# The output projection of a decoder layer in seven products of quarters per 1024 columns

## The chip, the cores and the metric

The kernel runs on one core of a Trainium2 chip. The metric is the device time of one execution in microseconds (us). [...]

## The reference, cut to what matters

One layer of a decoder on 512 tokens of width 2048. `D_IN` is 7184 columns, `w_out` is 2048 x 2048, all in float32.

```python
h = rms_norm(x, norm_g) * (1 + scale) + shift            # scale, shift, gate from c @ w_ada
z = h @ w_in
u_a, v_a, g_a, q_b, k_b, v_b, g_b, f_b = jnp.split(z, pts, axis=-1)
y_a = chunked_spatial_gating(gelu(u_a), gelu(v_a), ...) * silu(g_a)      # branch A, 1024 wide
y_b = forgetting_attention(q_b, k_b, v_b, f_b, b_f) * silu(g_b)          # branch B, 16 heads, 1024 wide
y = jnp.concatenate([y_a, y_b], axis=-1) @ w_out
return rms_norm(x + gate * y, final_g)
```

## The kernel before

**Precision.** Every float32 operand of a large product is split in two parts: `hi`, a rounded copy written by ACT (`split`, L65, or `w_tile`, L117), and `lo`, the source minus `hi`, written by DVE (or by POOL where `eng`/`loeng` says so). A product of a and b is three matmuls: hi·hi, lo·hi and hi·lo. A weight tile is therefore: a DMA into a `raw` tile (four buffers in all), an ACT copy into `whi`, a subtraction into `wlo` (two buffers each), and then the matmuls that use it.

**Tiles.** The activations lie with channels on the 128 partitions: `hh[k]`, `hl[k]` are block k (of 16) of h, 128 x 512 tokens. `mm_cols` makes 128 output columns x 512 tokens, `mm_toks` 128 tokens x up to 512 columns. A PSUM bank holds 128 x 512 sums; there are four of kind `mm`, and four that small work and attention share (`x`).

**Order of the program.** A first stage (L358) makes u_A and most of g_A while `w_ada` arrives. Then come groups of columns: `v_group` (v_B), `qk_group` and `g_group` (g_B) for four heads at a time, u = 0 to 3. Then the values of branch A (`va`, L689), the rest of its gate (`ga`, L764) and the output projection (L808).

Work that is not a large product hangs on two lists. `tick()` (L133) is called after each weight tile: it takes one entry of `slots` (the attention of the four heads before, later the mixing of branch A: `norm_half`, `mix_head`, `split_y`) and one entry of `fillers` (`gate_step`: POOL multiplies and adds up the adaLN gate, L584). The scheduler then sets the order of each engine's stream from the dependencies and priorities; weight tiles have a raised priority.

**Output projection.** For each of three groups of 512 columns, eight weight tiles of two channel blocks each (128 x 2 x 512) meet all four token tiles: 24 matmuls of 128 x 512 per weight tile. The weights of the fourth group are loaded ahead (`load_w3`) and used token tile by token tile (L823), so that the final norm of one token tile runs under the matmuls of the next. `wo_evac` multiplies by the gate (DVE, from PSUM), adds x (DVE), squares (ACT) and multiplies by `final_g` (DVE). The last lines scale by the norm and write out.

Of the kernel before, what the change touches and what calls it, by code (L numbers as in the profile page):

```python
# [27 lines left out]
def trunk_kernel(  # L28
# [281 lines left out]
    for kb in range(KB):  # L310
# [5 lines left out]
        xk = act.tile([P, S], F32, tag="y", name=f"xT{kb}")  # L316
# [32 lines left out]
    def new_y(b):  # L349
        y[b] = act.tile([P, S], F32, tag="y", name=f"y{b}")  # L350
# [111 lines left out]
    def attention_slots(u):  # L462
# [62 lines left out]
        def values(i):  # L525
# [16 lines left out]
            nc.vector.scalar_tensor_tensor(tm[a], op[a], 0.5, tm[a], ALU.mult, ALU.add)  # L542
            nc.vector.tensor_tensor(y[8 + b][a], tm[a], sgb[b][a], ALU.mult)
# [61 lines left out]
    bias2 = gp_.tile([P, 8, P], F32, name="bias2")  # L605
# [66 lines left out]
    v_group(0)  # L672
    qk_group(0)
    g_group(0)
    for u in range(1, 4):
        if u == 1:
            fillers.append(spatial_weights)
            for g in range(4):
                for i in range(8):
                    fillers.append(lambda g=g, i=i: gate_step(g, i))  # L680
                    if g and i == 2:
                        fillers.append(lambda g=g: gate_sum(g - 1))
            fillers.extend([lambda: None] * 3 + [lambda: gate_sum(3)])
# [60 lines left out]

    yh, yl = [None] * KB, [None] * KB

    def split_y(k):
        yh[k] = act.tile([P, S], F32R, tag="hh", name=f"yh{k}")
        yl[k] = act.tile([P, S], F32R, tag="hl", name=f"yl{k}")
        split(yh[k], yl[k], y[k], nc.gpsimd if k in (1, 3, 5, 7) else None)  # L750

    norm_half(0)
    c_ = lambda f, *a: (lambda: f(*a))
    slots.extend([
        [],
        [c_(mix_head, 0), c_(mix_head, 1)],
        [c_(mix_head, 2), c_(mix_head, 3)],
        [c_(norm_half, 1)],
        [c_(split_y, 0), c_(split_y, 1)],
        [c_(mix_head, 4), c_(mix_head, 5), c_(split_y, 2), c_(split_y, 3)],  # L760
        [c_(mix_head, 6), c_(mix_head, 7), c_(split_y, 4), c_(split_y, 5)],
        [c_(split_y, 6), c_(split_y, 7)],
    ])
# [112 lines left out]
```

## Time and profile before

| | |
|---|---|
| median of 3 runs | 920.67 us (920.17 to 920.79) |
| the profiled execution | 922.11 us, of which the span is 920.4 us |
| busy in the span | PE 898.9, DVE 528.7, ACT 412.4, POOL 326.4 us |
| mean granted clock of PE | 0.988 |
| read and written | 142.74 MB, mean 155 GB/s |

Busy time of PE counts a matmul from its start to its modelled end; consecutive matmuls overlap, so the pace has to be read from the distance between starts. All rows of the profile are of the one profiled execution, whose span is 0.3 us under the median.

### The profile page before, as it was taken

Reading aid. Unit: us, or ns where it says so; the run is one execution under the profiler, and the core shown is the slowest. Engines: PE = TensorE matmul, PEld = TensorE weight load, DVE = VectorE, ACT = ScalarE, POOL = GpSimd, SP = SyncE. Lnnn points to the kernel's source line nnn. Section 1 sums busy time; section 2 is a strip of 40 time slices with the busy share of each in tenths; the row PEclk is TensorE's granted clock in tenths of the full one; section 3 lists DMA queues with packets and bytes.
Section 4 is the critical chain, followed back from the end, with each engine's and each line's share of the span. In section 5 each row is a group of like instructions: output and inputs, shape, how many; then the busy total and the mean of one; then the engine's idle time right before and its main releaser. Section 6 shows DMA issues by size and latency. Waiting matters only on the chain.

```text
span 920.4 us, 12414 instructions
## 1 busy us (share of the span) xinstructions
PE 898.9 (98%) x4504; PEld 763.0 (83%) x4504; DVE 528.7 (57%) x886; ACT 412.4 (45%) x724; POOL 326.4 (35%) x238
## 2 busy tenths in 40 slices
PE   6999999999999999999999999999999999999995
PEld 4888888898888878988889888998888888888884
DVE  5678888364644685656645644555525884355522
ACT  5553323535464653654546544665514423233211
POOL 1366555531004997687897800000000230000000
PEclk8899999999999999999999999999999999999999
DMA  9999995234333454444556423223233233455222
GB/s 341 352 353 355 354 302 189 76 89 136 94 114 115 130 170 145 154 150 127 160 172 179 144 81 107 78 70 92 71 107 97 81 125 105 149 180 196 69 104 92
DMA packets 113821, 142.74 MB, mean 155 GB/s; under 512 B 8400, under 2 KB 85408, under 8 KB 113248
## 3 DMA queue, kind: packets, MB, share of 16 engines
q1 hardware_dynamic: 113328, 141.39, 48.5%
q8 instruction: 35, 0.57, 0.2%
q10 hardware_dynamic: 432, 0.57, 0.2%
q14 instruction: 26, 0.21, 0.1%
HBM read 137.54 MB, written 4.19 MB: 154 GB/s over the span
## 4 chain that ended last, share of the span: by engine, by line
PE 95%; DMA 2%; issue 1%; DVE 1%; ACT 0%; SPq 0%; POOLq 0%; POOL 0%; ACTq 0%; DVEq 0%
PE s L145 6%; PE s L147 6%; PE s L146 6%; PE wo L156 5%; PE wo L154 5%; PE wo L155 5%; PE vb L155 3%; PE vb L156 3%; PE vb L154 3%; PE k L145 3%; PE k L147 3%; PE gb L145 3%; PE gb L146 3%; PE k L146 3%; PE va L156 3%; PE gb L147 3%
## 5 line engine op out<-in xcount | busy, mean ns | idle before, releaser
L593 POOL TENSOR_SCALAR gate<-gate,sc 128x512 f32<-128x512 f32 x60 | 104.4, 1750 | 37.4 <-DMA gate<-in_w_ada_dram 34.5
L130 POOL TENSOR_TENSOR wlo_st<-raw_st,whi_st 128x1024 fp32r<-128x1024 f32 (+3 forms) x36 | 68.5, 1904 | 59.6 <-ACT whi_st L129 55.7
L145 PE MATMUL s<-hh,whi_st 128*128 128x512 f32 x224 | 88.0, 396 | 1.4 <-ACT hh L267 1.4
L146 PE MATMUL s<-hl,whi_st 128*128 128x512 f32 x224 | 88.1, 393 | 0.0
L594 POOL TENSOR_TENSOR gate<-gate,gate 128x512 f32<-128x512 f32 x60 | 86.5, 1442 | 2.1
L244 DVE SCALAR_TENSOR_TENSOR acc<-ada,sc,acc 128x512 f32<-128x512 f32 x98 | 73.9, 755 | 5.8 <-DMA ada<-in_w_ada_dram 3.1
L147 PE MATMUL s<-hh,wlo_st 128*128 128x512 f32 x224 | 76.4, 395 | 0.0
L154 PE MATMUL wo<-whi_wo,yh 128*128 128x512 f32 x192 | 74.8, 390 | 0.0
L155 PE MATMUL wo<-whi_wo,yl 128*128 128x512 f32 x192 | 74.7, 389 | 0.0
L155 PE MATMUL vb<-whi_vb,hl 128*128 128x256 f32 (+1 forms) x256 | 72.1, 287 | 0.0
L154 PE MATMUL vb<-whi_vb,hh 128*128 128x256 f32 (+1 forms) x256 | 71.8, 286 | 0.0
L156 PE MATMUL wo<-wlo_wo,yh 128*128 128x512 f32 x192 | 70.0, 390 | 0.0
L156 PE MATMUL vb<-wlo_vb,hh 128*128 128x256 f32 (+1 forms) x256 | 67.7, 285 | 0.0
L91 POOL TENSOR_TENSOR rsv<-rsv,nhalf 128x1 f32<-128x1 f32 x4 | 4.6, 1150 | 166.1 <-DVE rsv L90 166.1
L129 ACT ACTIVATE whi_st<-raw_st 128x1024 fp32r<-128x1024 f32 (+3 forms) x36 | 31.2, 870 | 66.3 <-PE s L146 40.9
L841 POOL TENSOR_TENSOR sfin<-sfin,nhalf 128x1 f32<-128x1 f32 x4 | 2.2, 549 | 149.0 <-DVE sfin L838 149.0
L145 PE MATMUL k<-hh,whi_k 128*128 128x512 f32 x128 | 51.1, 399 | 1.8 <-DVE q L445 1.8
L145 PEld LDWEIGHTS s<-hh,whi_st 128*128 128x128 f32 x224 | 42.6, 191 | 10.1 <-ACT hh L267 1.5
L146 PE MATMUL q<-hl,whi_q 128*128 128x512 f32 x128 | 50.7, 396 | 0.0
L145 PE MATMUL q<-hh,whi_q 128*128 128x512 f32 x128 | 50.4, 394 | 0.0
L146 PE MATMUL gb<-hl,whi_gb 128*128 128x512 f32 x128 | 50.3, 393 | 0.0
L145 PE MATMUL gb<-hh,whi_gb 128*128 128x512 f32 x128 | 50.3, 393 | 0.0
(227 smaller groups left out, 2363.8 us busy)
## 6 DMA issues: line engine op xcount, KB each, us to landing
ada<-in_w_ada_dram SPq DMA_DIRECT2D x128, 256.0 KB
gate<-in_w_ada_dram SPq DMA_DIRECT2D x32, 512.0 KB
raw_wo<-in_w_out_dram SPq DMA_DIRECT2D x24, 512.0 KB
raw_q<-in_w_in_dram SPq DMA_DIRECT2D x16, 512.0 KB
raw_k<-in_w_in_dram SPq DMA_DIRECT2D x16, 512.0 KB
raw_gb<-in_w_in_dram SPq DMA_DIRECT2D x16, 512.0 KB
raw_va<-in_w_in_dram SPq DMA_DIRECT2D x16, 512.0 KB
raw_st<-in_w_in_dram SPq DMA_DIRECT2D x21, 384.0 KB
```

Source lines behind the costliest of these rows:

```text
L91: nc.gpsimd.tensor_tensor(dst, dst, nhalf[:, 0:1], ALU.pow)
L129: nc.scalar.activation(hi, raw, AF.Copy)
L130: (loeng or nc.vector).tensor_tensor(lo, raw, hi.bitcast(F32), ALU.subtract)
L145: nc.tensor.matmul(pt, hi[:, j, cs], hh[k], start=(k == first), stop=False)
L146: nc.tensor.matmul(pt, hi[:, j, cs], hl[k], start=False, stop=False)
L147: nc.tensor.matmul(pt, lo[:, j, cs], hh[k], start=False, stop=(k == last))
L154: nc.tensor.matmul(o, ah[k][:, tsl], hi[:, j, :], start=(k == first), stop=False)
L155: nc.tensor.matmul(o, al[k][:, tsl], hi[:, j, :], start=False, stop=False)
L156: nc.tensor.matmul(o, ah[k][:, tsl], lo[:, j, :], start=False, stop=(k == last))
L244: nc.vector.scalar_tensor_tensor(sb if kk == KB - 1 else a, ga[:, j], col, a, ALU.mult, ALU.add)
L593: nc.gpsimd.tensor_scalar(ga[:, j], ga[:, j], sc[:, kk : kk + 1], None, ALU.mult)
L594: nc.gpsimd.tensor_tensor(a, a, ga[:, j], ALU.add)
```

## The change

**The projection in quarters.** Split y by tokens (first 256, last 256) and by channels (branch B's 1024, branch A's 1024), and w_out by the same channels and by two groups of 512 columns. A plain product of 2 x 2 quarters takes eight products of quarters; the scheme used takes seven, with sums and differences of the quarters on both sides. One run of it (`unit(u)`) makes 1024 columns (groups g1 = 2u and g2 = 2u+1), and there are two. Each product is four weight tiles of two channel blocks, and each tile serves two token tiles: 12 matmuls per tile, 48 per product.

| product | left side (activations) | weights, per tile |
|---|---|---|
| p1, into banks V | `A11`: branch B, first tokens | one tile of w_out |
| p7, into Z | `S3`: branch B, last minus first | difference T of two tiles |
| p6, into X | `S2` = S3 + branch A, last tokens | a tile minus T |
| p5, into Z | `S1` = S2 + branch B, first | a tile minus T |
| p2, into V | `A12`: branch A, first | one tile |
| p4, into X | `A22`: branch A, last | T minus the tile of p2 |
| p3, into Z | `S4`: branch A, first, minus S2 | one tile |

The sums of activations are made by POOL (`split_b`, `sums`), in place of the tiles `y`, and split once more. The differences of weights (`minus`) are made half by DVE, half by POOL; where a tile is used as loaded (p1, p2, p3) one of its two `lo` halves goes to POOL. Results are copied or added out of PSUM (`c1`, `c7`, `u2`, `u3`), multiplied by the gate (`gated`), x is added by POOL (`residual`), and the squares go to ACT. p1 of both units comes first, then the rest of unit 0, then unit 1, whose p3 is done token tile by token tile at the end.

**Branch A earlier.** `va_products` now stands right behind the first stage, and its mixing in the slots of `v_group(0)`. g_B of the last four heads moves behind `ga`. The gate of heads 12 to 15 is multiplied in later (`late`).

The diff, cut to its core:

```diff
+    def va_products(): ...        # the former loop over va, as a function
+    fillers.append(spatial_weights)
+    va_products()
+    slots.extend([
+        [c_(norm_half, 0)],
+        [c_(mix_head, 0), c_(mix_head, 1)],
+        [c_(mix_head, 2), c_(mix_head, 3)],
+        [c_(norm_half, 1)],
+        [c_(mix_head, 4), c_(mix_head, 5)],
+        [c_(mix_head, 6), c_(mix_head, 7)],
+    ])
     v_group(0)
     ...
-        g_group(u)
+        if u < 3:
+            g_group(u)
...
+    def split_b(i):
+        b = y[8 + i]
+        nc.gpsimd.tensor_tensor(b[:, hi_half], b[:, hi_half], b[:, lo_half], ALU.subtract)
+        split_y(8 + i)
+    def sums(i):
+        b, a = y[8 + i], y[i]
+        nc.gpsimd.tensor_tensor(b[:, hi_half], b[:, hi_half], a[:, hi_half], ALU.add)
+        nc.gpsimd.tensor_tensor(b[:, lo_half], b[:, lo_half], b[:, hi_half], ALU.add)
+        ...
+        split(sh_[i], sl_[i], b)
+        nc.gpsimd.tensor_tensor(b[:, lo_half], a[:, lo_half], b[:, hi_half], ALU.subtract)
+        s4[i] = act.tile([P, 2, H], F32R, name=f"s4_{i}", tag="ya", bufs=8)
+        split(s4[i][:, 0], s4[i][:, 1], b[:, lo_half])
...
+    def wsplit(src, name, eng=None):
+        ...
+        for j in range(2):
+            split(hi[:, j, :], lo[:, j, :], src[:, j, :], eng if j else None)
+        return hi, lo
+    def mm_part(bank_, kind, i, tt, hi, lo, begin, end):
+        h_, l_ = lhs(kind, i, tt)
+        nc.tensor.matmul(bank_, h_, hi, start=begin, stop=False, skip_group_check=True)
+        nc.tensor.matmul(bank_, l_, hi, start=False, stop=False, skip_group_check=True)
+        newest_mm[0] = nc.tensor.matmul(bank_, h_, lo, start=False, stop=end, skip_group_check=True)
+    def residual(rr, t, g, src=None, eng=None):
+        xr = pb.tile([P, 512], F32, name=f"xr{g}_{t}", tag="sgB", bufs=3)
+        nc.sync.dma_start(xr, x[0, t * P : (t + 1) * P, g * 512 : (g + 1) * 512])
+        (eng or nc.gpsimd).tensor_tensor(rr, rr, xr, ALU.add)
+        return xr
+    def piece(rr, t, g, fin=True):
+        xr = residual(rr, t, g)
+        squares(rr, t, g, xr)          # ACT; xr is free only after it
+        if fin:
+            nc.vector.tensor_tensor(rr, rr, fgs[g], ALU.mult)
...
+        def w_raw(half, g, name):
+            return lambda i: wsplit(raw(half, g, name, i), f"{name}_{u}_{i}", nc.gpsimd)
+        def minus(dst, a, b):
+            for j in range(2):
+                (nc.gpsimd if j else nc.vector).tensor_tensor(
+                    dst[:, j, :], a[:, j, :], b[:, j, :], ALU.subtract
+                )
+            return dst
...
+        product(V, "A11", w_raw(1, g1, "p1"), True, range(3))
+        yield
+        product(V, "A11", w_raw(1, g1, "p1"), True, [3])
+        ...
+        yield
+        product(Z, "S3", w_p7, True)
+        ...
+        product(X, "S2", w_p6, True)
+        ...
+        both(lambda t: nc.gpsimd.tensor_tensor(u3[t], u2[t], c7[t], ALU.add))
+        both(lambda t: nc.gpsimd.tensor_tensor(c7[t], c7[t], c1[t], ALU.add))
+        product(Z, "S1", w_p5, True)
+        ...
+        for i in range(4):
+            product(V, "A12", w_p2, False, [i])
+            product(X, "A22", w_p4, False, [i])
+        ...
+            product(Z, "S4", w_raw(0, g2, "p3"), False)       # unit 0; unit 1: by token tile
```

Where the instructions stand now is shown at three places. The first is POOL. Before, these are the last rows of its stream that work on whole tiles: the four values of branch A (`vl`) and four blocks of y, and from there to the end of the kernel only four instructions of 128x1 (`sfin`):

```order
L91 TENSOR_TENSOR rsv_6452<-rsv_6452,nhalf 128x1
L67 TENSOR_TENSOR yl_6764<-y_1730,yh_6763 128x512
L67 TENSOR_TENSOR vl_1_6663<-va_1_5764,vh_1_6662 128x512
L67 TENSOR_TENSOR vl_1_6668<-va_1_5766,vh_1_6667 128x512
L67 TENSOR_TENSOR vl_1_6673<-va_1_5768,vh_1_6672 128x512
L67 TENSOR_TENSOR vl_1_6678<-va_1_5770,vh_1_6677 128x512
L67 TENSOR_TENSOR yl_6834<-y_1734,yh_6833 128x512
L67 TENSOR_TENSOR yl_6904<-y_1738,yh_6903 128x512
L67 TENSOR_TENSOR yl_6942<-y_1811,yh_6941 128x512
L841 TENSOR_TENSOR sfin<-sfin,nhalf 128x1 x4
```

Now POOL works through the whole projection; this piece is unit 0 around the end of p6 (`ta`, `tb`, `tc` hold T, L912 is `minus`, L973 and L974 the sums into `u3` and `c7`, L869 is `residual`):

```order
L912 TENSOR_TENSOR tc_7065<-b_0_3_7254,tc_7065 128x512
L912 TENSOR_TENSOR p_0_0_7286<-p_0_0_7286,ta_7063 128x512
L912 TENSOR_TENSOR p_0_1_7308<-p_0_1_7308,ta_7063 128x512
L912 TENSOR_TENSOR p_0_2_7330<-p_0_2_7330,tb_7064 128x512
L912 TENSOR_TENSOR p_0_3_7352<-p_0_3_7352,tc_7065 128x512
L973 TENSOR_TENSOR u_0_7278<-u_0_7276,c_0_7182 128x512
L973 TENSOR_TENSOR u_1_7279<-u_1_7277,c_1_7183 128x512
L912 TENSOR_TENSOR ta_7063<-p_0_0_7390,ta_7063 128x512
L974 TENSOR_TENSOR c_0_7182<-c_0_7182,c_0_7023 128x512
L974 TENSOR_TENSOR c_1_7183<-c_1_7183,c_1_7024 128x512
L912 TENSOR_TENSOR ta_7063<-p_0_1_7430,ta_7063 128x512
```

POOL had nothing of 128x512 behind the mixing; from p1 to the end it now has 82 instructions of 128x512 and 10 of 128x256, every one with two inputs in SBUF.

The second place is DVE. Before, in the second group of the projection, one subtraction of 128x1024 per weight tile (24 matmuls):

```order
L130 TENSOR_TENSOR wlo_wo_12_7170<-raw_wo_12_7167,whi_wo_12_7169 128x1024
L130 TENSOR_TENSOR wlo_wo_14_7200<-raw_wo_14_7197,whi_wo_14_7199 128x1024
L130 TENSOR_TENSOR wlo_wo_0_7230<-raw_wo_0_7227,whi_wo_0_7229 128x1024
L130 TENSOR_TENSOR wlo_wo_2_7260<-raw_wo_2_7257,whi_wo_2_7259 128x1024
L67 TENSOR_TENSOR w3l_7418<-raw_w_0_7415,w3h_7417 128x1024
```

Now p7 and the start of p6 of unit 0 (an `x2` is the two halves of one tile):

```order
L912 TENSOR_TENSOR ta_7063<-b_0_1_7100,b_0_1_7102 128x512
L67 TENSOR_TENSOR wlo_p_0_1_7107<-ta_7063,whi_p_0_1_7106 128x512 x2
L912 TENSOR_TENSOR tb_7064<-b_0_2_7134,b_0_2_7136 128x512
L67 TENSOR_TENSOR wlo_p_0_2_7141<-tb_7064,whi_p_0_2_7140 128x512 x2
L912 TENSOR_TENSOR tc_7065<-b_0_3_7158,b_0_3_7160 128x512
L912 TENSOR_TENSOR ta_7063<-b_0_0_7188,ta_7063 128x512
L67 TENSOR_TENSOR wlo_p_0_3_7165<-tc_7065,whi_p_0_3_7164 128x512 x2
```

Three instructions of 128x512 with two inputs in SBUF now stand for 12 matmuls, where one of 128x1024 stood for 24.

The third place is SP between p3 of unit 0 (`p_0_*_76xx`) and p7 of unit 1 (`b_1_*`). Before, in the same part of the program, the loads of x (`xr`) stood among the weights of the projection too:

```order
L790 DMA xr_0_7075<-in_x_dram 128x512
L790 DMA xr_1_7081<-in_x_dram 128x512
L123 DMA raw_wo_8_7107<-in_w_out_dram 128x2x512
L790 DMA xr_2_7087<-in_x_dram 128x512
L790 DMA xr_3_7093<-in_x_dram 128x512
L123 DMA raw_wo_10_7137<-in_w_out_dram 128x2x512
```

Now:

```order
L868 DMA xr_3_7571<-in_x_dram 128x512
L825 DMA b_1_0_7675<-in_w_out_dram 128x2x512
L868 DMA xr_0_7660<-in_x_dram 128x512
L825 DMA b_1_0_7677<-in_w_out_dram 128x2x512
L868 DMA xr_1_7665<-in_x_dram 128x512
L825 DMA b_1_1_7699<-in_w_out_dram 128x2x512
L868 DMA xr_2_7964<-in_x_dram 128x512
L825 DMA b_1_1_7701<-in_w_out_dram 128x2x512
```

Each `xr` has one of three buffers (tag `sgB`), free again when ACT has squared an earlier piece, so the weights of p7 behind it are issued only after the pieces of unit 0 have gone through POOL and ACT.

More of the change, by code (lines that the diff above doesn't have):

```diff
@@ L315, in trunk_kernel @@
             )
-        xk = act.tile([P, S], F32, tag="y", name=f"xT{kb}")
+        xk = act.tile([P, S], F32, tag="ya" if kb < 8 else "yb", bufs=8, name=f"xT{kb}")
         with ExitStack() as es:
@@ L349, in new_y @@
     def new_y(b):
-        y[b] = act.tile([P, S], F32, tag="y", name=f"y{b}")
+        y[b] = act.tile([P, S], F32, tag="ya" if b < 8 else "yb", bufs=8, name=f"y{b}")
     def evac_g(b, pt, pool):
@@ L670, in qk_group @@
         slots.extend(attention_slots(u))
[L672 to L683, printed above, removed]
-        g_group(u)
-        qk_group(u)
-        v_group(u)
@@ L743, in mix_head @@
         nc.vector.tensor_tensor(y[h], y[h], mt, ALU.mult)
-    yh, yl = [None] * KB, [None] * KB
+    fillers.append(spatial_weights)
[8 more added lines that the diff above has]
+    ])
+    v_group(0)
+    heads_tiles()
+    qk_group(0)
+    g_group(0)
+    for u in range(1, 4):
+        if u == 1:
+            for g in range(4):
+                for i in range(8):
+                    fillers.append(lambda g=g, i=i: gate_step(g, i))
+                    if g and i == 2:
+                        fillers.append(lambda g=g: gate_sum(g - 1))
+            fillers.extend([lambda: None] * 3 + [lambda: gate_sum(3)])
+        if u < 3:
+            g_group(u)
+        qk_group(u)
+        v_group(u)
+    H = S // 2
+    yh, yl = [None] * KB, [None] * KB
+    sh_, sl_, s4 = [None] * 8, [None] * 8, [None] * 8
+    lo_half, hi_half = slice(0, H), slice(H, S)
+    def split_b(i):
+        b = y[8 + i]
+        nc.gpsimd.tensor_tensor(b[:, hi_half], b[:, hi_half], b[:, lo_half], ALU.subtract)
+        split_y(8 + i)
     def split_y(k):
@@ L823, in trunk_kernel @@
[L823 to L836 removed]
+    fga = pb.tile([P, 2, 512], F32, name="fga", tag="fs")
@@ new lines, in trunk_kernel, with wtile, wget @@
+    nc.sync.dma_start(
+        fga.rearrange("p a n -> p (a n)"),
+        final_g[0:1024].rearrange("(a n) -> a n", a=1).broadcast_to([P, 1024]),
+    )
+    fgs = {0: fga[:, 0, :], 1: fga[:, 1, :]}
+    def wtile(name):
+        return wp.tile([P, 2, 512], F32, tag="raw", name=name, bufs=4)
+    def wget(dst, half, g, i):
+        k = 8 * half + 2 * i
+        nc.sync.dma_start(dst, wout_r[:, k : k + 2, g * 512 : (g + 1) * 512])
+        return dst
+    def wsplit(src, name, eng=None):
+        hi = wp.tile([P, 2, 512], F32R, tag="whi", name=f"whi_{name}")
+        lo = wp.tile([P, 2, 512], F32R, tag="wlo", name=f"wlo_{name}")
+        for j in range(2):
+            split(hi[:, j, :], lo[:, j, :], src[:, j, :], eng if j else None)
+        return hi, lo
@@ new lines, in product, with gated @@
+    def product(banks, kind, weights, begin, steps=range(4)):
+        for i2 in steps:
+            with tc.high_priority(offset=WPRI):
+                hi, lo = weights(i2)
+            for j in range(2):
+                for tt in range(2):
+                    i = 2 * i2 + j
+                    mm_part(banks[tt], kind, i, tt, hi[:, j, :], lo[:, j, :], begin and i == 0, i == 7)
+            tick()
+    def gated(rr, src, g):
+        nc.vector.tensor_tensor(rr, src, gate[:, g, :], ALU.mult)
@@ L852 @@
+    units = [unit(0), unit(1)]
+    for z in units + units:
+        next(z)
+    for z in units:
+        for _ in z:
+            pass
 _INS = ["x", "c", "norm_g", "w_ada", "b_ada", "w_in", "ln_v_g", "ln_v_b", "w_s", "b_s", "b_f", "w_out", "final_g"]
```

295 lines of the change are left out of this document (180 added, 115 removed).

## The prediction

> **What bounds the kernel now.** I read the page's shares first, then the chain of waits.
>
> ```profile
> PE 898.9 (98%) x4504; PEld 763.0 (83%) x4504; DVE 528.7 (57%) x886; ACT 412.4 (45%) x724; POOL 326.4 (35%) x238
> PE 95%; DMA 2%; issue 1%; DVE 1%; ACT 0%; SPq 0%; POOLq 0%; POOL 0%; ACTq 0%; DVEq 0%
> ```
>
> The chain is PE for 95% of the span, so time goes where matmuls go. Their pace comes from the chain in order of time: the same row returns once per weight tile of 24 matmuls.
>
> ```profile
> 771.18 0.45 PE wo L156 x2
> 776.62 0.45 PE wo L156 x2
> ```
>
> 5.44 us for 24 is 0.2267 us per 128x512 matmul. Then the groups by shape, for counts and unit prices, and two stretches of the span:
>
> ```profile
> L154 PE MATMUL wo<-whi_wo,yh 128*128 128x512 f32 x192 | 74.8, 390 | 0.0
> L833 PE MATMUL wo<-w3h,yh 128*128 128x512 f32 x64 | 24.9, 389 | 0.0
> L785 DVE TENSOR_TENSOR r<-wo,gate 128x512 f32<-128x512 f32 x16 | 10.9, 688 | 29.9 <-PE wo L835 24.5 <-PE wo L156 5.4
> L66 ACT ACTIVATE yh<-y 128x512 fp32r<-128x512 f32 x16 | 10.0, 629 | 22.0 <-DVE y L743 19.2 <-PE ga L147 2.6
> ...
> L130 POOL TENSOR_TENSOR wlo_st<-raw_st,whi_st 128x512 fp32r<-128x512 f32 x4 | 5.1, 1281 | 15.0 <-ACT whi_st L129 13.7 <-PE s L147 1.4
> L130 POOL TENSOR_TENSOR wlo_st<-raw_st,whi_st 128x384 fp32r<-128x384 f32 x4 | 4.1, 1015 | 3.3 <-ACT whi_st L129 3.3
> ```
>
> ```profile
> 40.00:60.00 20.00, 20.00 (x94) 16.67 (x93) 14.41 (x23) 12.04 (x21) 11.28 (x8) 1.00 1.08 354
> ...
> 760.00:780.00 20.00, 20.00 (x90) 16.58 (x89) 8.25 (x10) 5.00 (x7) 1.81 (x1) 1.00 0.33 112
> ```
>
> In the projection PE is full, DVE busy 8.25 of 20 us and POOL 1.81. PE has no slack; what it is fed by has plenty. Whether that survives is the question.
>
> **Removed: matmuls.** Three kinds (hi·hi, lo·hi, hi·lo) of 192 + 64 are 768. Seven products of 48 in two units are 672. 96 x 0.2267 = 21.8 us less on PE: 920.4 - 21.8 = 898.6 us, if nothing else waits.
>
> **Added: elementwise work.** The split copies on ACT (112 of 0.629, 70 us) have the whole projection of 152 us to hide in, and the DMAs (56 weight tiles of 0.52 MB, 29 MB) ask for under 200 GB/s where 354 were moved between 40 and 60 us: both cost nothing by themselves. DVE and POOL are different, and how they run together has to be read instruction by instruction. First DVE, then POOL, in order of time:
>
> ```profile
> 718.74 1.89 DVE L67 TENSOR_TENSOR yl<-y,yh 128x512 fp32r<-128x512 f32 x3
> 734.37 2.16 DVE L130 TENSOR_TENSOR wlo_wo<-raw_wo,whi_wo 128x1024 fp32r<-128x1024 f32 x1
> 738.24 1.26 DVE L743 TENSOR_TENSOR y<-y,mt 128x512 f32<-128x512 f32 x1
> 739.42 1.78 DVE L355 SCALAR_TENSOR_TENSOR y<-sgA,y 128x512 f32<-128x512 f32 x1
> 741.13 0.86 DVE L740 SCALAR_TENSOR_TENSOR mt<-mix,cols,mt 128x256 f32<-128x256 f32 x2
> 756.71 1.64 DVE L740 SCALAR_TENSOR_TENSOR mt<-mix,cols,mt 128x256 f32<-128x256 f32 x4
> 758.28 1.28 DVE L743 TENSOR_TENSOR y<-y,mt 128x512 f32<-128x512 f32 x2
> ```
>
> ```profile
> 735.41 6.95 POOL L67 TENSOR_TENSOR vl<-va,vh 128x512 fp32r<-128x512 f32 x4
> 744.26 1.29 POOL L67 TENSOR_TENSOR yl<-y,yh 128x512 fp32r<-128x512 f32 x1 [1.89 <-ACT yh L66]
> ```
>
> Alone, a DVE instruction with two SBUF inputs takes 0.69 us and, back to back, 0.60 (1.89 for three, 1.28 for two); one of POOL takes 1.28. Together they don't run side by side. L355 took 1.78 and L743 1.26 while POOL had its four `vl`, and those took 6.95 instead of 5.12. L740, which reads PSUM and one SBUF tile, took 0.43 each both at 741.13, under POOL, and at 756.71, without it. So two SBUF inputs on DVE and POOL's two-input subtraction exclude each other; with one input from PSUM they don't.
>
> How much is lost in an alternation? L130 ends at 736.53, the last `vl` at 742.36: 5.83 us for four POOL instructions (5.12) and two of DVE, so 0.36 per inserted DVE instruction. A pair costs between 1.28 + 0.36 = 1.64 and 1.28 + 0.60 = 1.88.
>
> [...]
>
> **The sum of the shared path.** From p1 on, DVE has 156 instructions of 128x512 and 5 of 128x256 with two SBUF inputs (differences of weights, `lo` halves, sums, gates of SBUF tiles, `final_g`): 156 x 0.60 + 5 x 0.36 = 95 us. POOL has 82 of 128x512 and 10 of 128x256 (0.75 by the slope between 1.281 and 1.015). Full price: 82 x 1.28 + 10 x 0.75 = 112.5. Set between DVE instructions, a POOL one adds 1.64 - 0.60 = 1.04, and about 0.5 for the half: 90. So DVE alone needs 95, POOL alone 112, PE 152 us: each would hide. The sum is 185 to 208, and does not.
>
> About 7.5 of it stands ahead of p1's first matmul (the rows in front of DVE's and POOL's second `lo` of p1), and 9.5 beside unit 1's p3, which takes PE 10.9 us and needs only weights that are split by then. The other 168 to 191 us stand against 13 products of 48 x 0.2267 = 10.88, or 141.5 us. PE has to wait 27 to 49 us. I take the middle, 38: the instructions are mixed about two of DVE to one of POOL, so some handovers overlap and some are runs of one engine.
>
> DVE's additions and gates that read PSUM (about 20 x 0.688 = 14 us) run under POOL and cost nothing as long as POOL holds the path anyway.
>
> **Idle time of that path.** It isn't busy all the time. The place I worked through by hand is unit 0's p3 into unit 1's p7, counted from the last matmul of p4: POOL's seven instructions up to the last `residual` (L869) and the DVE work between them take 12 us; ACT squares, SP is let past the last `xr` at about 13, the fourth raw buffer comes free at 15, the second tile of p7 lands near 19 and is split at 21.5, and p7 ends near 31, where PE needs 21.8. The path's own sum there is 30 to 34, so the queue on SP costs little more than the path already does. What waits there is SP's whole stream behind `xr`: the weights of p7, then PE. For all such gaps I allow 0 to 16 us (a tenth of the path's time) and take 8.
>
> **The end.**
>
> ```profile
> 900.00:921.00 21.00, 10.81 (x48) 8.63 (x46) 5.35 (x10) 4.12 (x8) 1.09 (x2) 0.88 0.27 101
> ```
>
> Before, 9.6 us follow the last matmul (900 + 10.81 to 920.4), and the other token tiles are long done. Now token tiles 2 and 3 are scaled and written inside the last product, and DVE's stream has the pieces of `c1` and `c7` ahead of token tile 0's gate (some 16 instructions, 8 us, with POOL's `residual` and ACT's squares between them). By adding these up the last tile starts 2 to 3 us late; I take 2.5, between 0 and 4.
>
> **Branch A moved.** Its matmuls only change place. What could show is the first mixing, behind 32 matmuls of `v_group(0)`.
>
> ```profile
> 200.00:220.00 20.00, 20.00 (x147) 19.29 (x146) 7.16 (x14) 7.06 (x18) 9.80 (x20) 1.00 0.54 148
> ...
> 707.14 0.39 PE L145 MATMUL ga<-hh,whi_ga 128*128 128x512 f32 x1
> ...
> 710.90 1.28 DVE L67 TENSOR_TENSOR vl<-va,vh 128x512 fp32r<-128x512 f32 x2
> ```
>
> At 20/147 us each, 32 matmuls cover 4.4 us. Before, the normalised values were there by 710.90, 3.8 us after the values' last product (707.14). It is close: 0 to 3 us, taken as 1. The gate's POOL work moves back with it by about the 87 us of the values (384 x 0.2267), and still ends before `ga`.
>
> **The sum.** 898.6 + 38 + 8 + 2.5 + 1 = 948 us of span; the median stands 0.3 above the span: 949 us. From the terms' ends: 926 to 971.
>
> **The rivals.** *PE stays full (faster).* For it speaks that in 760 to 780 DVE and POOL together were busy 10 of 20 us, and that each alone fits. It needs the shared path to cost under 141.5 + 17 = 158.5 us, about 1.3 us per pair instead of 1.64 to 1.88, which no row of the stretch 734 to 743 shows. Then 898.6 + 0 to 6: about 902 us.
>
> *Part of the work runs ahead (between).* Sums, `minus` and raw tiles may be done earlier than I place them, in `ga` and g_B, where POOL has room. 20 us more of the path taken out of the projection would give about 912 to 926.
>
> *The clock falls (slower still).*
>
> ```profile
> PE k L145 <- DVE q L445: 1.8, 1, 1.8
> ...
> 346.00:348.00 2.00, 2.00 (x7) 1.57 (x6) 2.00 (x1) 1.32 (x4) 2.00 (x3) 0.52 0.00 0
> 348.00:350.00 2.00, 2.00 (x7) 1.52 (x7) 1.31 (x4) 1.08 (x2) 1.21 (x1) 0.62 0.86 234
> ```
>
> The one wait of PE between weight tiles, 1.8 us at 345, was followed by a granted clock of 0.52 and 0.62 for 2 us each: 0.96 + 0.76 = 1.7 us lost on top. If each of the 14 products starts with such a wait, that is 24 us more, up to 972 or, from the upper end, 985 us and over. Against it: most waits should be under a microsecond per tile (46 us over 56 tiles), and a PE that isn't the bound can lose time unseen. [...]
>
> **Chances.** The shared path as reckoned, 926 to 971: 0.66. With the clock, 972 to 990: 0.16. In between, 905 to 926: 0.08. PE full, near 902: 0.10. The range 926 to 985 holds the first and most of the second, about 0.8. A difference under 0.2% (1.8 us) can hardly be told from none: faster 0.14 (PE full, and half of the case between), same 0.02, slower 0.84.
>
> **What would show it.** Right: idle time of PE before `wo` matmuls put down to `lo` tiles on DVE and POOL; DVE's `lo` of 128x512 at 0.9 us or more in the mean instead of 0.69; POOL and DVE together near full from p1 on; all of the loss after p1. The queue on SP: a gap in p7 of unit 1. The clock: stretches of the projection under 1.00. Wrong, if DVE's halves keep 0.69 beside a busy POOL, or if PE stays at 20 of 20 us in the projection.

## The result and the profile after

The changed kernel takes 966.55 us (median of four runs, 964.69 to 969.12) against 920.73 us for the kernel before on the same chip: ratio 1.048, 95% interval 1.041 to 1.054, slower. The forecast was 949 us with an own range of 926 to 971. The profiled execution took 969.12 us, its span 967.4 us; all rows below marked "after" are of it. Several kernels here run some 9 us longer in single executions, at a mean granted clock 0.01 lower (the kernel before took 920.2 to 920.8 us three times and 928.9 once), so a median of four can lie between two groups of times, as the 950.40 of experiment 2 does.

The page's shares and the chain of waits, after (PE runs the matrix products, DVE and POOL the elementwise work, ACT activations and copies; SP issues the DMAs):

```profile
PE 898.8 (93%) x4408; PEld 749.5 (77%) x4408; DVE 657.7 (68%) x986; ACT 454.1 (47%) x827; POOL 496.2 (51%) x354
PE 75%; DVE 14%; issue 4%; DMA 2%; POOL 2%; ACT 1%; POOLq 0%; DVEq 0%; ACTq 0%; SPq 0%
```

PE has 96 matmuls fewer and is no less busy, which already says that its matmuls got slower or stood apart; DVE, which held 1% of the chain, holds 14%. Where PE waits from 700 us on (engine, line waited at, who let it go; us in total, times, longest):

```profile
PE woZ L851 <- DVE wlo_p L67: 13.2, 9, 3.4
PE woX L851 <- DVE wlo_p L67: 8.7, 9, 2.1
PE woV L849 <- DVE sgA L346: 6.4, 1, 6.4
PE woV L851 <- DVE wlo_p L67: 5.3, 4, 1.6
PE woZ L849 <- ACT whi_p L66: 5.1, 5, 1.6
PE woV L851 <- POOL wlo_p L67: 2.8, 1, 2.8
PE o L540 <- DVE ptl L67: 1.7, 1, 1.7
PE gb L147 <- DVE wlo_gb L130: 0.8, 1, 0.8
```

L851 is the matmul that needs the `lo` half (`mm_part`). The groups by shape show what that half costs now, on DVE and on POOL:

```profile
L67 DVE TENSOR_TENSOR wlo_p<-p,whi_p 128x512 fp32r<-128x512 f32 x36 | 47.1, 1323 | 2.2 <-ACT whi_p L66 1.8 <-PE woV L851 0.3
L67 DVE TENSOR_TENSOR wlo_p<-ta,whi_p 128x512 fp32r<-128x512 f32 x24 | 24.0, 1021 | 1.0 <-ACT whi_p L66 0.9
L67 POOL TENSOR_TENSOR wlo_p<-p,whi_p 128x512 fp32r<-128x512 f32 x20 | 32.1, 1604 | 6.1 <-ACT whi_p L66 6.1
```

1.02 to 1.32 us on DVE instead of 0.69, 1.60 on POOL instead of 1.28. The two streams in order of time show why: four of DVE, four of POOL.

```profile
853.99 1.78 DVE L880 TENSOR_TENSOR c<-c,fga 128x512 f32<-128x512 f32 x1
855.69 1.75 DVE L67 TENSOR_TENSOR wlo_p<-p,whi_p 128x512 fp32r<-128x512 f32 x1
857.36 1.77 DVE L880 TENSOR_TENSOR c<-c,fga 128x512 f32<-128x512 f32 x1
859.05 1.78 DVE L67 TENSOR_TENSOR wlo_p<-p,whi_p 128x512 fp32r<-128x512 f32 x1
860.75 0.68 DVE L912 TENSOR_TENSOR ta<-b,b 128x512 f32<-128x512 f32 x1
...
853.48 1.73 POOL L67 TENSOR_TENSOR wlo_p<-p,whi_p 128x512 fp32r<-128x512 f32 x1
855.18 1.71 POOL L869 TENSOR_TENSOR c<-c,xr 128x512 f32<-128x512 f32 x1
856.85 1.73 POOL L912 TENSOR_TENSOR ta<-b,b 128x512 f32<-128x512 f32 x1
858.54 1.74 POOL L67 TENSOR_TENSOR wlo_p<-p,whi_p 128x512 fp32r<-128x512 f32 x1
```

Both engines look busy without a gap, and both advance by one instruction every 1.69 us ((859.05 - 853.99) / 3). As soon as POOL has nothing, at 860.75, DVE's takes 0.68. A pair therefore costs 1.69 us, inside the forecast's 1.64 to 1.88, and a POOL instruction between DVE's adds 1.69 - 0.60 = 1.09.

**Where the 47 us come from.** p1's first matmul starts at 747.31 and the last one of the kernel ends at 955.4. The rows are that matmul, the stretch ahead of it and the whole stretch of the projection (us, then busy time of PE, PEld, DVE, ACT and POOL, granted clock, DMA share, GB/s):

```profile
747.31 0.79 PE L849 MATMUL woV<-whi_p,yh 128*128 128x512 f32 x1 [6.37 <-DVE sgA L346]
...
720.00:740.00 20.00, 17.52 (x81) 14.20 (x81) 18.59 (x21) 12.55 (x26) 20.00 (x18) 1.00 0.16 52
747.30:955.40 208.10, 172.68 (x672) 129.53 (x672) 185.09 (x192) 85.22 (x162) 139.09 (x92) 0.94 0.46 151
```

In the last row's 208.1 us PE was busy 172.7, at a mean granted clock of 0.94; 672 matmuls at 0.2267 are 152.3.

| part | us | worked out from |
|---|---|---|
| matmuls removed | -21.8 | 96 x 0.2267 |
| p1 starts late | +10.6 | 747.3, against 910.8 (last matmul before) - 768 x 0.2267 = 736.7 |
| PE idle from p1 on | +35.4 | 208.1 - 172.7 |
| clock below 1.00 | +10.4 | 0.06 x 172.7 |
| restarts behind the stops | +10.0 | 172.7 - 10.4 - 152.3 |
| end behind the last matmul | +2.4 | 12.0 (967.4 - 955.4), against 9.6 |
| sum | +47.0 | 967.4 - 920.4 |

What a restart costs is an estimate from two numbers: a matmul row lasts 0.39 us and the pace is 0.2267, so the last matmul ahead of a stop, which no next one overlaps, adds 0.16 us. In the stretches of full clock PE stands idle 31 times between two matmuls, which makes 5.0 us of such ends, and 36 more matmuls start late without idle time to show for it, 3.9 us. The clock is printed with two digits, so its row and that of the restarts are good to about 1 us each. The table says where PE's time went; it isn't a list of prices, since with a full clock part of the 10.4 us could have come back as idle time. No run separates that.

### The profile page after: what moved, and what is told of

Same layout as the page of the kernel before. It is cut to its first block, busy times and chain, and to the rows that moved or that the text cites. A ratio compares the mean times of both kernels' runs of the same rounds, so it can differ in the third digit from the quotient of the medians.

```text
span 967.4 us, 12726 instructions
## 1 busy us (share of the span) xinstructions
PE 898.8 (93%) x4408; PEld 749.5 (77%) x4408; DVE 657.7 (68%) x986; ACT 454.1 (47%) x827; POOL 496.2 (51%) x354
## 4 chain that ended last, share of the span: by engine, by line
PE 75%; DVE 14%; issue 4%; DMA 2%; POOL 2%; ACT 1%; POOLq 0%; DVEq 0%; ACTq 0%; SPq 0%
PE s L145 5%; PE s L147 5%; PE s L146 5%; DVE wlo_p L67 5%; PE vb L155 3%; PE vb L156 3%; PE vb L154 3%; PE q L145 3%; PE q L146 3%; PE q L147 3%; PE k L147 3%; PE va L156 3%; PE va L154 3%; PE va L155 3%; PE k L146 3%
## 5 line engine op out<-in xcount | busy, mean ns | idle before, releaser
L605 POOL TENSOR_TENSOR gate<-gate,gate 128x512 f32<-128x512 f32 x60 | 92.0, 1535 | 1.9
L145 PE MATMUL s<-hh,whi_st 128*128 128x512 f32 x224 | 88.0, 396 | 1.4 <-ACT hh L267 1.4
L156 PE MATMUL vb<-wlo_vb,hh 128*128 128x256 f32 (+1 forms) x256 | 71.0, 286 | 0.0
L145 PE MATMUL q<-hh,whi_q 128*128 128x512 f32 x128 | 50.5, 394 | 2.0 <-DVE mt L739 2.0
L67 DVE TENSOR_TENSOR ptl<-p,pth 128x512 fp32r<-128x512 f32 (+1 forms) x64 | 43.0, 696 | 13.5 <-ACT pth L66 12.2
L145 PE MATMUL k<-hh,whi_k 128*128 128x512 f32 x128 | 50.7, 396 | 0.0
L147 PE MATMUL gb<-hh,wlo_gb 128*128 128x512 f32 x128 | 49.8, 393 | 0.8 <-DVE wlo_gb L130 0.8
L145 PEld LDWEIGHTS s<-hh,whi_st 128*128 128x128 f32 x224 | 42.6, 191 | 10.1 <-ACT hh L267 1.5
L145 PE MATMUL gb<-hh,whi_gb 128*128 128x512 f32 x128 | 50.4, 394 | 0.0
L154 PE MATMUL va<-whi_va,hh 128*128 128x512 f32 x128 | 50.3, 393 | 0.0
L487 DVE CUSTOM_DVE_ANT_0 s<-s,cmask 128x128 f32<-128x128 f32 (+1 forms) x64 | 31.0, 505 | 28.2 <-PE s L486 27.3
```

The lines of the kernel that those rows point to most:

```text
L67: (eng or nc.vector).tensor_tensor(lo, src, hi.bitcast(F32), ALU.subtract)
L145: nc.tensor.matmul(pt, hi[:, j, cs], hh[k], start=(k == first), stop=False)
L147: nc.tensor.matmul(pt, lo[:, j, cs], hh[k], start=False, stop=(k == last))
L154: nc.tensor.matmul(o, ah[k][:, tsl], hi[:, j, :], start=(k == first), stop=False)
L156: nc.tensor.matmul(o, ah[k][:, tsl], lo[:, j, :], start=False, stop=(k == last))
L605: nc.gpsimd.tensor_tensor(a, a, ga[:, j], ALU.add)
```

## The experiments

**Theory**, my reading of the turns above (1.69 us a pair): DVE and POOL share one path for SBUF inputs, and the sum of their work on it is longer than PE's. **Rivals:** the load of each engine by itself; two buffers are too few; the transfers or SP's queue; the new order. All but 7 start from the changed kernel; 9 also puts branch A back where it stood before.

**1. POOL's weight halves on DVE.**

```diff
-            return lambda i: wsplit(raw(half, g, name, i), f"{name}_{u}_{i}", nc.gpsimd)
+            return lambda i: wsplit(raw(half, g, name, i), f"{name}_{u}_{i}")
-                (nc.gpsimd if j else nc.vector).tensor_tensor(
+                nc.vector.tensor_tensor(                    # minus; likewise p2 and the pre-split p3
```

> All of POOL's halves of the weights (20 lo halves of p1, p2 and p3, 4 of the pre-split p3, 32 differences) go to DVE; POOL keeps the residuals, the sums and the yl tiles. Theory (DVE and POOL share one path for two SBUF inputs): the path's sum falls from 185 to 208 us to 129 for DVE (95 + 56 x 0.60) plus 35 to 41 for what stays on POOL, 163 to 170; less the 17 us that lie ahead of p1 or beside the last p3 that is 146 to 153 against 141.5 us of PE. The time falls to 928 to 942 us. Rival (it is work per engine that counts, and DVE is the fuller one): DVE has 143 us with its PSUM reads against 152 us of PE and gets a third more to do, so the time stays at 960 or rises. Rival (queue on SP and depth of buffers): little change, 955 to 966.

942.13 us (939.24 to 952.66), ratio to before 1.024 (1.016 to 1.031), 24 us less than with the change. DVE got 56 instructions more and its `lo` halves became shorter:

```profile
L67 DVE TENSOR_TENSOR wlo_p<-p,whi_p 128x512 fp32r<-128x512 f32 x54 | 51.8, 996 | 1.9 <-ACT whi_p L66 1.9
L67 DVE TENSOR_TENSOR wlo_p<-tc,whi_p 128x512 fp32r<-128x512 f32 x12 | 7.9, 681 | 1.2 <-ACT whi_p L66 1.2
```

The last matmul starts at 925.2 instead of 955.0. By the pair's price 56 x (1.09 - 0.60) = 27 us leave the path; the last matmul moves by 30 between the two profiled executions, the medians by 24. That the fuller engine would be the bound is refuted; the time lies just above the theory's upper end.

**2. POOL reads one input.** The second is left out of the computation.

```diff
-        (eng or nc.gpsimd).tensor_tensor(rr, rr, xr, ALU.add)
+        nc.gpsimd.tensor_copy(rr, xr)        # likewise lo halves, minus, the sums into u3 and c7
```

> POOL's subtractions and additions of 128x512 from p1 on (lo halves, differences, residuals, the sums into u3 and c7) become POOL copies of 128x512 that read one SBUF tile; their place, their number and what waits for them stay, only the second input is left out of the computation. Theory (two SBUF inputs on DVE and two on POOL exclude each other, one on POOL doesn't hold DVE): DVE's lo halves go back from 1.0 to 1.3 us to about 0.69, DVE and POOL fit side by side, PE waits for little and the clock stays up: 905 to 930 us. Rival (POOL itself is too slow, 1.28 us and more per half in a chain with ACT and DVE that has two buffers): 945 us or more. Rival (any access of POOL to SBUF holds DVE): no change, about 966.

950.40 us (945.22 to 954.69), ratio 1.030 (1.023 to 1.037): a miss. The time lies in the range of the first rival, POOL's own slowness, but PE waits for a half from POOL only once in the projection, for 0.3 us, and 18.5 us for halves from DVE. DVE's halves fell only to 0.75 to 0.87 us. The streams say why (two of DVE, two of POOL):

```profile
866.30 1.09 DVE L67 TENSOR_TENSOR wlo_p<-tc,whi_p 128x512 fp32r<-128x512 f32 x1
867.31 1.09 DVE L921 TENSOR_TENSOR tb<-b,tb 128x512 f32<-128x512 f32 x1
...
866.83 1.04 POOL L919 COPY p<-ta 128x512 f32<-128x512 f32 x1
867.81 1.07 POOL L875 COPY u<-xr 128x512 f32<-128x512 f32 x1
```

A POOL copy with one SBUF input holds up DVE's two-input instruction too: 1.09 us here, where a row of DVE takes 0.69 with POOL idle (853.04). It is only shorter (0.61 us at 843.17, with DVE idle): a pair is 1.01 us, so it adds 0.41 instead of 1.09. My distinction by POOL's second input was wrong. Still, by this estimate 80 such instructions at 1.09 - 0.41 make the path 54 us shorter, more than the 45 us that PE lost in idle time and restarts, and the time falls by only 16. The stretches show a part of what is left:

```profile
820.00:840.00 20.00, 19.36 (x84) 15.21 (x83) 12.07 (x17) 10.88 (x23) 7.33 (x9) 1.00 0.38 128
840.00:860.00 20.00, 10.89 (x35) 7.83 (x33) 7.75 (x12) 4.87 (x11) 4.54 (x6) 0.77 0.67 233
```

PE is nearly full up to 840, then half empty with DVE and POOL idle as well: that is p7 of unit 1, where every step needs two weight tiles. DVE waits there for the tile of its first difference:

```profile
L921 DVE TENSOR_TENSOR ta<-b,b 128x512 f32<-128x512 f32 x4 | 2.9, 723 | 13.0 <-DMA b<-in_w_out_dram 13.0
```

**3. p7 with half of its loads**, tried on the changed kernel and, later, on the one-input kernel.

```diff
-            minus(T[i], raw(1, g2, "b12", i), raw(0, g2, "b22", i))
+            b12 = raw(1, g2, "b12", i)
+            minus(T[i], b12, b12[:, ::-1, :])
```

> p7 loads one raw tile per step instead of two and takes the difference of its two halves, which leaves the second tile out of the computation; the work of DVE, POOL, ACT and PE is the same, 8 loads of 0.52 MB are gone. Theory (forecast: the shared path alone, loads are hidden): no change, 963 to 968 us. Rival (p7 asks for 8 tiles in 10.9 us, 385 GB/s, and that together with four raw buffers holds it up): p7 of both units loses its waits, 950 to 960 us.

> POOL's work as copies with one SBUF input, and p7 with one raw tile per step instead of two (the second tile and POOL's second inputs are left out of the computation). Theory: with the shared path out of the way the next bound in p7 is the transfers (two tiles per step, 385 GB/s at PE's pace; DVE stood 13 us at the first difference waiting for its tile), so here this change shows, unlike in the kernel with the shared path full: 920 to 935 us. Rival (what is left there is POOL's or ACT's latency, not the transfers): 942 to 950 us.

On the changed kernel: 969.12 us against 966.55, ratio to before 1.052 (1.048 to 1.056), no gain. On the one-input kernel: 937.88 us against 950.40, and the last matmul at 921.9 instead of 931.3; 3 us above what was expected. So the transfers of p7 are a second bound, hidden as long as the first one holds. The same 20 us with half of the loads on the one-input kernel:

```profile
840.00:860.00 20.00, 16.20 (x63) 12.34 (x61) 15.21 (x24) 5.39 (x11) 11.08 (x8) 0.91 0.62 215
```

**4. Three buffers for the split weights in unit 0.**

```diff
+        third[0] += 1
+        if third[0] % 3 == 0 and "_0_" in name:
+            both_ = pb.tile([P, 4, 512], F32R, tag="wsp", name=f"w3rd_{name}")
+            hi, lo = both_[:, 0:2, :], both_[:, 2:4, :]
```

> In unit 0 every third weight tile of a product gets a buffer of its own for hi and lo (three deep instead of two); unit 1 as it was. Theory (throughput of the shared path): a deeper buffer evens out single waits but doesn't make the path faster: 0 to 5 us less than after the change, 961 to 967. Rival (two buffers are too few, the waits are latency from raw tile to lo): unit 0's waits fall by half or more, and with the clock 10 to 18 us go: 948 to 956.

965.64 us, ratio 1.046 (1.040 to 1.053): within the theory's 0 to 5 us. A third buffer in unit 0 didn't make the path faster.

**5. The loads of x off SP's queue.**

```diff
-        nc.sync.dma_start(xr, x[0, t * P : (t + 1) * P, g * 512 : (g + 1) * 512])
+        nc.scalar.dma_start(xr, x[0, t * P : (t + 1) * P, g * 512 : (g + 1) * 512])
```

> The 16 loads of x for the residuals are issued by ACT instead of SP, so the loads of weights behind them don't wait. Theory (forecast: the queue on SP costs little more than the path does): 0 to 5 us less, 961 to 967 us. Rival (SP stands 42 us at these loads and holds up the weights of the next product): 10 us and more, below 957 us.

966.47 us, ratio 1.051 (1.048 to 1.055): nothing. SP had stood 42 us at these loads, and what waited behind it was not what PE waited for.

**6. The sums of y held back** behind POOL's `lo` halves of p1.

```diff
+    def held(i):
+        with ExitStack() as es:
+            es.enter_context(tc.issue_after(newest_lo[0].ins))
+            sums(i)
```

> The sums of blocks of y (S1, S2, S4) are held back behind POOL's lo halves of p1 instead of running ahead of p1. Theory (the path's work is conserved): p1 starts 8 to 10 us earlier, and the 25 us of sums come back as waits in p7 and p6: 960 to 972 us. Rival (the late start of p1 is only the order on DVE's queue): the 10 us and their slow clock are won, 952 to 957 us.

969.10 us, ratio 1.053 (1.051 to 1.054). p1 no longer waits (it starts at 735.2), and the stretches show the loss in p7 instead:

```profile
740.00:760.00 20.00, 17.70 (x76) 13.60 (x75) 11.96 (x11) 9.97 (x18) 17.13 (x13) 1.00 0.55 186
760.00:780.00 20.00, 11.60 (x36) 7.71 (x34) 16.62 (x16) 8.44 (x16) 20.00 (x19) 0.82 0.39 138
```

The last matmul starts at 955.06, with the change at 954.97. The 10.6 us ahead of p1 and the waits behind it are one account: the path's work is conserved.

**7. Branch A moved, the projection plain.** The order of the changed kernel, with the projection of the kernel before.

```diff
+    va_products()                  # ahead of v_group(0), the mixing in its slots
     v_group(0)
     ...
+    col_group([(G0 + 768, 256)], ..., "ga")
+    g_group(3)                     # behind ga
```

> The projection in plain form as before the change (four groups, the last by token tile); branch A's values and mixing behind the first stage, ga ahead of the last g_B, as after the change. Theory (forecast): moving branch A costs 0 to 3 us, 919 to 924. Rival (the 10 us by which p1 starts late after the change come from the new order itself): 928 to 932.

926.11 us, ratio 1.0045 (1.0006 to 1.0084), 4 us or 0.6 to 7.7: midway between theory and rival. The trace has a wait of 1.9 us at the first mixing (`q` L145 behind DVE's `mt`), but the 1.8 us that the kernel before waits at 345 are gone, so the two cancel. The other wait is 2.4 us at the first matmul of the projection behind ACT's `yh`, which is of my arrangement of the splits there; 3.4 us at a clock of 0.50 follow it, another 1.7 us lost. If these 4 us belong to that arrangement, which no run separates, moving branch A costs about nothing.

**8. Residuals and sums on DVE too** (on top of 1; POOL keeps only the sums of y and `yl`).

```diff
-        (eng or nc.gpsimd).tensor_tensor(rr, rr, xr, ALU.add)
+        nc.vector.tensor_tensor(rr, rr, xr, ALU.add)       # likewise the sums into u3 and c7
```

> As the kernel with the halves of the weights on DVE, and the residuals and the sums into u3 and c7 on DVE too; POOL keeps the sums of y and yl. Theory (shared path): 24 instructions cost the path 0.6 instead of 1.04 to 1.28 us, 10 to 16 us less on the path; but DVE alone then has 129 + 14 us of two-SBUF-input work and 14 of PSUM reads against 152 us of PE, nearly all of its time: 930 to 940 us. Rival (work per engine counts, and DVE is the full one): 945 us or more.

936.67 us, ratio 1.015 (1.009 to 1.020), as expected. With POOL out of the way DVE is full by itself, over 16 of 20 us in every stretch of the projection and up to

```profile
800.00:820.00 20.00, 19.75 (x87) 15.89 (x87) 20.00 (x34) 9.45 (x18) 0.00 (x0) 1.00 0.44 157
```

and by the pair's price whatever is moved back to POOL would cost the path 1.09 instead of 0.60 us. At that, 24 instructions should have given 12 us; 5 are measured. What is left over the time before are the late p1 (PE waits 5.9 us for `sgA` here too), waits of 12.6 us in the projection, and the clock.

**9. Seven products for half of the columns.** If the sum is the bound, the scheme pays where its elementwise work is spread over more matmuls. Columns 0 to 1023 are plain, from the same operands:

```diff
+    def plain(g):
+        for n, k in enumerate((8, 10, 12, 14, 0, 2, 4, 6)):
+            hi, lo = w_tile([(g * 512, 512)], k, 2, src=wout_r, name=f"wo{g}_{k}")
+            for banks, kind in ((W, "S3" if k >= 8 else "A22"), (V, "A11" if k >= 8 else "A12")):
+                ...
+            if n == 3:      # A11 B1, which S3 lacks for the lower tokens, is kept and added to W
+                ...
+                nc.scalar.activation(top[t], V[t], AF.Copy)
```

> Seven products for columns 1024 to 2047 only; columns 0 to 1023 as plain products (two groups of 512, same operands: S3 and A22 for the lower token tiles, whose missing A11 B1 is taken from a copy of the upper ones). Sums of y and the first differences of weights are made while the plain groups run, all halves of weights on DVE, branch A where it stood before the change. 48 matmuls fewer than before: 10.9 us. Theory (shared path, its work spread over the whole projection): in the one unit DVE and POOL have 50 us of lo halves, 14 of differences and 20 to 25 of pieces against 76 us of PE, so PE waits 2 to 8 us there; the end is 2.6 us longer: 912 to 920 us. Rival (in seven products the waits come from something else than the path's sum: two buffers, the queue on SP, the clock): 20 us of waits in the unit remain, as in one unit after the change: 926 to 934 us.

927.17 us, ratio 1.008 (1.006 to 1.011): on the rival's side. But the trace has 9.5 us of idle time of PE in the whole projection, where the rival asks for 20 in the unit alone. It named two faults that the theory itself knows: the sums crowded into the first plain group, and POOL's residuals beside DVE in the unit. Both were taken away:

```diff
-        nc.gpsimd.tensor_tensor(b[:, hi_half], b[:, hi_half], a[:, hi_half], ALU.add)
+        es.enter_context(tc.issue_after(newest_wlo[0].ins))     # one set per step, on DVE
+        nc.vector.tensor_tensor(b[:, hi_half], b[:, hi_half], a[:, hi_half], ALU.add)
...
-        xr = residual(rr, t, g)
+        xr = residual(rr, t, g, eng=nc.vector)
```

> As the kernel with seven products for columns 1024 to 2047 only, with the sums of y moved to DVE and held back so that one set is made per step from the second plain group's start on (where DVE was busy 4 of 10 us), and all residual additions on DVE; POOL has no two-input work of 128x512 behind the mixing but yl. Theory (shared path): the 4 us of waits in the first plain group go, and each residual costs the path 0.6 instead of 1.04 us; in the unit p6 to p4 still need 46 to 50 us of DVE against 43.5 of PE: 5 to 8 us of waits stay. 918 to 924 us. Rival (the sums were no part of the loss): 925 to 928 us.

922.19 us, ratio 1.0013 (0.998 to 1.004): the same as before, as expected. PE now ended earlier, at 906.6 against 910.8, but 14.6 us followed instead of 9.6:

```profile
910.00:920.00 10.00, 0.00 (x0) 0.00 (x0) 2.15 (x5) 2.75 (x6) 0.55 (x1) 0.50 0.95 354
```

The engines do little there (DVE 2.15, ACT 2.75 of 10 us); the output is being written, at 354 GB/s. The last kernel finishes token tiles 2 and 3 first and makes p7's differences earlier:

```diff
-    ] + [[], [], []] + [[c_(sums, i)] for i in range(8)] + [[c_(prep_t, i)] for i in range(4)])
+    ] + [[], [], []] + [[c_(sums, i)] + ([c_(prep_t, i - 3)] if 3 <= i < 7 else []) for i in range(8)])
-        both(lambda t: piece(c1[t], t, g1))
-        both(lambda t: piece(c7[t], 2 + t, g1))
+        ...                       # c7's pieces and scale_out of token tiles 2 and 3
+        both(c1_piece)            # issue_after c7's
```

> As the kernel before it (seven products for columns 1024 to 2047 only, sums spread), with two changes. The first differences for p7 are made in the middle of the second plain group, so that their 8 loads no longer stand with those of p1 (324 GB/s, DMA share 0.96 there); and behind p4 the token tiles 2 and 3 are finished ahead of branch c1, so that their output is written while p3 runs. Theory: in the kernel before, PE ended 4 us ahead of the kernel before the change and gave 5 us back behind its last matmul, where all four token tiles' output (4.2 MB at 354 GB/s, 12 us) was written at once; with half of it written during p3 the end falls from 14.7 to 10 or 11 us, and p1 loses 2 to 4 us less: 914 to 918 us. Rival (the end is set by the chain of the last token tile, not by the writes): 919 to 922 us.

913.39 us (median of twelve, 912.97 to 922.61), ratio to before 0.994 (0.991 to 0.998), just under what was expected. It beats the kernel before and the changed one. In the second half of the projection PE is full again, DVE nearly so, POOL empty:

```profile
840.00:860.00 20.00, 20.00 (x89) 16.44 (x88) 18.13 (x26) 9.19 (x17) 0.00 (x0) 1.00 0.29 99
860.00:880.00 20.00, 19.12 (x82) 14.84 (x81) 20.00 (x31) 11.06 (x23) 0.00 (x0) 1.00 0.44 157
880.00:900.00 20.00, 19.73 (x87) 15.97 (x86) 19.05 (x40) 9.72 (x22) 2.00 (x2) 1.00 0.29 100
```

Its last matmul ends at 900.6; 48 matmuls fewer than before are 910.8 - 10.9 = 899.9. Nearly the whole saving is there, and 10.8 us follow (span 911.4). How much of the 9 us each of the two edits brought was not separated.

## Why the prediction was right and where it was wrong

- **Removed matmuls, 21.8 us:** right; in experiment 9 the last matmul ends 10.2 us earlier, of 10.9 that half of them are worth.
- **The shared path, 38 us, and its idle time, 8:** right. PE's idle time and the restarts from p1 on are 35.4 + 10.0 = 45.4 us against 46. The path itself bears it out: in the trace DVE's instructions with two SBUF inputs and POOL's together cover 192 of the 208 us from p1 on, where the forecast had 185 to 208, and leave 16 free, at the edge of the 0 to 16 allowed. That 45.4 meets 46 so closely is partly luck, since the path goes on while PE runs at a clock of 0.50 and the two can't be told apart. What the runs show of the cause is in 1, 2 and 8: work taken from POOL gave time back (24, 16 and 5 us), also where DVE got it instead; in 1 about the pair's price, in 2 and 8 less, because there the loads of p7 and DVE alone take over.
- **"About 7.5 of it stands ahead of p1" and costs nothing, and branch A 1 us:** this step was mis-sized, 10.6 us instead of 1. I looked only at p1's own `lo` halves. The scheduler let the sums of y run ahead into the last g_B group as well, where DVE was busy 18.59 and POOL 20.00 of 20 us (720 to 740), and DVE's stream had `sl` and `s` ahead of `sgA`, which p1's banks wait for. With the path full there, nothing ahead of p1 was free, and the sign "all loss after p1" was wrong with it. Experiment 6 shows that the two are one account.
- **The clock, set in a rival at 0.16:** it belonged in the sum. The waits are 0.6 us per weight tile, as I argued, but they come as some 30 stops of 1.2 us in the mean and up to 3.4 us, and the lower clock took 10 us of PE's time.
- **The end, 2.5 us:** right, 2.4.
- **Transfers "cost nothing by themselves":** right for this kernel (3), for the wrong reason. 200 GB/s is a mean; p7 takes 4.2 MB in 10.9 us, 385 GB/s, and was hidden only by the slower path (2 and 3: it shows once the path is shorter).
- **The signs:** DVE's `lo` at 0.9 us or more, waits put down to `lo` tiles, stretches of low clock and a gap in p7 of unit 1 all appeared; what made that gap in the changed kernel was not isolated, since neither p7's second tile (3) nor the loads of x (5) alone moved the time.
- **SP's queue "costs little more than the path already does":** right (5).

The 9.6 us at p1 and 10.4 us of clock, less 0.7 in the other terms, are the 19 us by which the span passed the forecast's 948. PE full, and work that runs ahead (the two faster rivals), did not happen: what ran ahead only filled the path earlier.

## What to carry to other kernels

Before work is moved to a second engine because both have room, look in the trace whether the two advance together or in turns: here the price is nearly the sum of both (1.69 us a pair, of 0.60 and 1.28), and the busy shares (DVE 89%, POOL 67% of the projection) hide it, since a row counts the time spent waiting for the other engine too (DVE's 1.78 us beside POOL's, 0.68 without). An algorithm that trades matmuls for elementwise work pays only as far as the elementwise sum fits beside the matmuls that remain; here the scheme for half of the columns, with the unit's elementwise work on DVE and the sums spread over the plain products, branch A back in its place and half of the output written earlier, turned 5% slower into 0.6% faster (0.2 to 0.9). And a bound that is taken away shows the next one (the loads of p7, the output at the end): look there before calling the first theory wrong.

## What the hardware showed that I had not expected

**POOL's multiplication by a column held DVE up too, but only near its start.** A copy of 128x512 with one SBUF input, 0.61 us long, added 0.41 us to DVE's two-input instruction (experiment 2). In the kernel before, POOL multiplies tiles by a column (L593, 1.57 us each where nothing is in the way), and DVE's subtraction of 128x1024 takes 1.22 us in the mean where POOL is idle. Three of these subtractions meet a multiplication (the POOL rows hold two each; the second of the last row starts at 448.48):

```profile
400.02 1.57 DVE L130 TENSOR_TENSOR wlo_gb<-raw_gb,whi_gb 128x1024 fp32r<-128x1024 f32 x1 [0.67 <-ACT whi_gb L129]
337.66 1.47 DVE L130 TENSOR_TENSOR wlo_k<-raw_k,whi_k 128x1024 fp32r<-128x1024 f32 x1 [0.52 <-ACT whi_k L129]
449.32 1.23 DVE L130 TENSOR_TENSOR wlo_k<-raw_k,whi_k 128x1024 fp32r<-128x1024 f32 x1 [0.47 <-ACT whi_k L129]
...
399.83 3.19 POOL L593 TENSOR_SCALAR gate<-gate,sc 128x512 f32<-128x512 f32 x2
337.37 3.20 POOL L593 TENSOR_SCALAR gate<-gate,sc 128x512 f32<-128x512 f32 x2 [0.38 <-DMA gate<-in_w_ada_dram]
446.94 3.34 POOL L593 TENSOR_SCALAR gate<-gate,sc 128x512 f32<-128x512 f32 x2
```

The first starts 0.19 us behind POOL's and takes 0.35 longer; the second starts 0.29 behind and takes 0.25 longer. Both sums are 0.54 us. The third starts 0.84 behind and isn't held at all. In the trace after the change two more (389.40 and 395.27) start 0.15 and 0.18 behind and take 0.39 and 0.36 longer, 0.54 again. One of the kernel before, at 314.80, starts 0.11 behind, right after other DVE instructions, and takes 1.21; there it was POOL's that took longer, 3.21 us. By these rows, as an estimate, the multiplication costs DVE at most 0.54 of its 1.57 us, where the copy costs 0.41 of its 0.61 and the two-input instruction 1.09 of its 1.28. The length of a POOL instruction didn't tell what it cost DVE.

**The length of one gap didn't decide the clock.** After the change, three restarts of PE, and the busy time of PE and the clock (the number behind the brackets) in stretches of 3.41 us around them:

```profile
765.22 0.73 PE L851 MATMUL woV<-wlo_p,yh 128*128 128x512 f32 x2 [2.84 <-POOL wlo_p L67]
908.13 1.22 PE L851 MATMUL woZ<-wlo_p,sh 128*128 128x512 f32 x2 [3.39 <-DVE wlo_p L67]
929.72 0.50 PE L851 MATMUL woX<-wlo_p,yh 128*128 128x512 f32 x1 [2.05 <-DVE wlo_p L67]
...
760.37:763.78 3.41, 2.01 (x9) 1.00 0.38 135
763.78:767.20 3.42, 1.98 (x9) 1.00 0.24 57
903.73:907.14 3.41, 1.01 (x5) 1.00 0.43 154
907.14:910.55 3.41, 2.42 (x6) 0.50 0.00 0
927.63:931.04 3.41, 1.36 (x7) 1.00 0.74 226
931.04:934.45 3.41, 3.41 (x9) 0.50 0.16 43
```

A gap of 2.84 us left the clock at 1.00, one of 2.05 us was followed by 0.50, and so was one of 3.39. The rows differ in where the gap lies. Between 60 us and the last matmul the clock of this trace changed ten times: down to 0.50 at 743.31, 873.01, 886.66, 907.14 and 931.04, back to 1.00 at 750.13, 879.84, 890.08, 913.97 and 934.45. The distance between any two of these points is a whole multiple of 3.41 us, and the stretches above are counted from them. The gap of 2.84 us lies across the end of a stretch, and PE is busy 2.01 and 1.98 us of the two that share it (59 and 58%); the gap of 2.05 us lies in one stretch and leaves 1.36 (40%), and the one of 3.39 leaves 1.01 (30%) of the stretch it begins in. The five falls stand behind stretches with PE busy 30 to 51% (1.01 to 1.75 us); the lowest stretch without a fall behind it, at 828.64, has 54% (1.85 us). The kernel before has one fall there, at 346.10, behind a stretch with PE busy 46% (1.58 us). The clock came back behind a stretch with PE busy 83% (2.82 us, at 746.72) and, the other five times, behind a full one.
